# Sample attention by head in four column groups, and state-space outputs with channels on the rows

## The chip, the cores and the metric

One core of a Trainium2 chip runs the whole step. TensorE (PE in the profile, PEld its weight loads) multiplies; VectorE (DVE), ScalarE (ACT) and GpSimd (POOL) work elementwise; SyncE (SP) issues every DMA, in order. The metric is device microseconds of one execution. The kernel before was timed three times: 2014.14, 2015.0 and 2017.74 us, median 2015.0.

## The reference, cut to what matters

One layer of an encoder with four groups of heads that read one normalised input, for a prompt of 1024 rows and a sample of 32 rows (with a cache of 2048 past keys). Two groups matter here.

Group B is attention without softmax. Per head, with z = scale · q·k for every key before the query:

```
log_keep = where(mask, log_sigmoid(-z), 0)
suffix   = reverse_cumsum(log_keep) - log_keep
w        = where(mask, exp(log_sigmoid(z) + suffix), 0)
out      = w @ v          # 8 heads x 64
```

Group A is a state-space scan in chunks (8 heads of 64 channels in 2 groups of 4 heads, state of 128). Per chunk, with `acum` the running sum of dt·a, `decay` the causal exp(acum_t - acum_s), and h the state carried in:

```
y     = einsum('bthn,bshn,btsh,bshp->bthp', cc, bc, decay, xdt)
y    += einsum('bthn,bhpn,bth->bthp', cc, h, exp(acum))
h_new = exp(last) * h + einsum('bshn,bsh,bshp->bhpn', bc, w_s, xdt)
```

Afterwards y gets d_skip · x, is gated and normed, and the four groups go through one output projection and a layer norm.

## The kernel before, in words

The prompt is worked in two halves of 512 rows (`h` = 0, 1); the 32 sample rows go with the first. The input projection is 48 column tiles (`col_tile`, lines 351 to 353: three products of split operands per k), and these matmuls are the steady load of TensorE. `ORDER` and `weave` set what goes beside them: the second part of each unit (the attention blocks, the scan chunks and so on) is a generator, of which `weave` runs one step after every so many column tile steps. `follow` gives how many steps a generator has, so that they are spread evenly. After that the Tile scheduler orders the instructions of each engine, and each engine runs its own in that order.

`b_sample(gq)` (two calls, for heads 0 to 3 and 4 to 7; a pair of heads shares the 128 rows of a q, k or v tile) goes over the keys in five blocks, first the 32 new ones (`blk` 4), then four of 512. Its scores `zs` (line 917) hold four heads x 32 queries on 128 rows: the q tile `qb` of a pair is 128 x 128 with zeros outside its heads' places, and the two pairs add into one PSUM tile. `stick` makes weights `w` of it on ACT and DVE; `back` turns them (line 890) and multiplies (line 896) with v as the stationary operand, 128 x 128 for both heads of a pair, against 64 columns of weights, of which half of each product is not used.

`a_unit(h, g)` works a group of 4 heads in chunks of 128 rows (4 per half, and chunk 4 of 32 rows for the sample in the first half: 18 chunks in all for two groups and two halves). `weights` prepares a chunk: `bca` is the running sum copied to all rows by a DMA, three transposes `px` (lines 566 to 568), `xd` = x·dt (and a second version on POOL, line 572), `pg` = B·C (line 577), and `L`, the decay matrix of four heads: DVE, exp on ACT (line 584), product with `gt` on POOL (line 585). `outputs`, one step later, has the rows of the chunk on the partitions: four matmuls with `L` as the stationary operand against 64 columns (line 597), C against the state of 256 columns (line 600), two DVE operations that scale the second by exp(acum) and add (lines 605, 607), and the state update `pst` (line 609). `turn`, another step later, transposes y to channels on the rows (line 624) and adds d_skip · x (line 626). The loop has nch + 2 steps, 7 in the first half and 6 in the second. A group's second unit in a half is woven with the next half's first attention unit, and in the second half with the output projection (`prev`).

Of the kernel before, what the change touches and what calls it, by code (L numbers as in the profile page):

```python
# [6 lines left out]
F32 = mybir.dt.float32  # L7
F32R = mybir.dt.float32r
AF = mybir.ActivationFunctionType
ALU = mybir.AluOpType  # L10
# [52 lines left out]
def step_kernel(ctx, tc, xp, xs, cst, wmss, wmg, bgate, win, wsm, wout, lng, lnb, ck, cv,  # L63
# [320 lines left out]
    def narrow(h):  # L384
# [95 lines left out]
        for c in range(nch):  # L480
# [11 lines left out]
            A.activation(col[0:n, c, 24:32], col[0:n, c, 0:8], AF.Exp)  # L492
# [35 lines left out]
    def a_unit(h, g):  # L528
# [27 lines left out]
        def weights(c, n, cc):  # L556
# [30 lines left out]
            return L, xd, bt, el  # L587

        def outputs(c, n, cc, L, xd, bt, el):
            first = h == 0 and c == 0  # L590
            Hc = H
            if c == 4:
                Hc = sp.tile([P, 256], F32, tag="hs", name=nm("hs"), bufs=1)
                nc.sync.dma_start(Hc, ssmT[:, g * 256:(g + 1) * 256])
            py = ZT("py")
            for hh in range(4):
                T.matmul(py[0:n, hh * 64:(hh + 1) * 64], L[0:n, hh, 0:n], xd[0:n, 0, hh * 64:(hh + 1) * 64],  # L597
                         start=True, stop=True)
            if not first:
                T.matmul(py[0:n, 256:512], tiles["C"][:, cc], Hc, start=True, stop=True)  # L600
            y = WK("ya", [P, 2, 256])
            if first:
                V.tensor_copy(y[0:n, 0, :], py[0:n, 0:256])
            else:
                V.tensor_tensor(g4(y[0:n, 1, :], 4), g4(py[0:n, 256:512], 4),
                                col[0:n, c, 24 + 4 * g:28 + 4 * g].to_broadcast([n, 4, 64]), op=ALU.mult)
                V.tensor_tensor(y[0:n, 0, :], y[0:n, 1, :], py[0:n, 0:256], op=ALU.add)
# [11 lines left out]
            return y  # L619

        def turn(n, cc, y):
            pt = ST("pyt")
            for j in range(2):
                T.transpose(pt[:, j * P:j * P + n], y[0:n, 0, j * P:(j + 1) * P], ident[0:n, 0:n])
            for j in range(2):
                V.scalar_tensor_tensor(yg[j][:, cc], tiles[f"x{j}"][:, cc], C("dsk", 2 * g + j),
                                       pt[:, j * P:j * P + n], op0=ALU.mult, op1=ALU.add)

        todo1 = todo2 = None
        for c in range(nch + 2):  # L630
            done = todo2
            todo2 = None
            if todo1:
                todo2 = (*todo1[1:3], outputs(*todo1))
                todo1 = None
# [5 lines left out]
            if done:  # L641
                turn(*done)
# [920 lines left out]
```

## Time and profile before

| | before |
|---|---|
| median of three runs | 2015.0 us |
| profiled execution, its own time | 2011.09 us |
| its span from first to last instruction | 2009.2 us |
| TensorE busy | 1916.5 us (95%) |
| DVE, ACT, POOL busy | 1341.6, 767.0, 272.7 us |
| mean granted TensorE clock | 0.989 of full speed |

The span is the time from the first to the last instruction; the execution's own time has 1.9 us around it. Busy times of TensorE count modelled ends of matmuls that overlap, so what a matmul costs is read from the distance between starts, not from its own duration. A float32 matmul shows as two records, each with a weight load; the split operands of the projection are one record each, a transpose too.

### The profile page before, as it was taken

The page shows a single profiled execution, that of the slowest core. Times are in us where ns is not written, and L with a number is a line of the kernel's source. Part 1 is how long each engine was busy: PE and PEld are TensorE (multiplying, and loading weights), DVE is VectorE, ACT ScalarE, POOL GpSimd, SP SyncE. Part 2 cuts the span into 40 slices and gives each one's busy share as a digit, 9 for nine tenths or more (in the row PEclk, how much of TensorE's full clock was granted, in tenths as well). Part 3 has the DMA queues.
Part 4 walks back from the last instruction along what each step waited for, and adds up shares of the span by engine and source line. Part 5 has one row for each costly group of instructions (what it writes and reads, how often), then busy time and mean ns, then how long its engine had stood idle before and what let it go on. Part 6 is the DMA issues. An engine that isn't in the chain of part 4 may idle for free. (4 is left out here: it accounts for less than half of the span.)

```text
span 2009.2 us, 31503 instructions
## 1 busy us (share of the span) xinstructions
PE 1916.5 (95%) x11956; PEld 1599.0 (80%) x11956; DVE 1341.6 (67%) x2610; ACT 767.0 (38%) x1278; POOL 272.7 (14%) x481
## 2 busy tenths in 40 slices
PE   3999999999999999999999999999999999998998
PEld 1578999998889999977787886777878676676787
DVE  4325667877956857876678779876857664355765
ACT  5212533334464434435444444533334421133321
POOL 1000111202211202331101011121111210000000
PEclk9999999999999999999999999999999999999998
DMA  9786344333443343644232332433433635457733
GB/s 320 260 282 226 119 127 127 118 121 121 138 145 119 105 117 101 175 126 139 91 113 94 113 101 85 122 99 102 126 99 101 210 107 184 151 190 239 226 128 131
DMA packets 162031, 291.38 MB, mean 145 GB/s; under 512 B 23836, under 2 KB 66076, under 8 KB 161880
## 3 DMA queue, kind: packets, MB, share of 16 engines
q1 hardware_dynamic: 161880, 289.37, 45.3%
q8 instruction: 94, 1.54, 0.3%
q14 instruction: 57, 0.47, 0.1%
HBM read 253.49 MB, written 35.82 MB: 144 GB/s over the span
## 5 line engine op out<-in xcount | busy, mean ns | idle before, releaser
L351 PE MATMUL ip<-uh,wh 128*128 128x272 f32 (+4 forms) x2368 | 775.8, 328 | 0.4 <-POOL uh L277 0.4
L352 PE MATMUL ip<-ul,wh 128*128 128x272 f32 (+4 forms) x2368 | 765.6, 323 | 0.0
L353 PE MATMUL ip<-uh,wl 128*128 128x272 f32 (+4 forms) x2368 | 764.1, 323 | 0.0
L326 ACT CAST wh<-wr 128x1024 fp32r<-128x1024 f32 (+1 forms) x257 | 268.3, 1044 | 671.2 <-PE ip L352 404.8
L327 DVE TENSOR_TENSOR wl<-wr,wh 128x1024 fp32r<-128x1024 f32 (+1 forms) x257 | 314.6, 1225 | 253.8 <-ACT wh L326 239.4
L351 PEld LDWEIGHTS ip<-uh,wh 128*128 128x128 f32 x2368 | 449.5, 190 | 38.9 <-issue 7.7
L352 PEld LDWEIGHTS ip<-ul,wh 128*128 128x128 f32 x2368 | 449.4, 190 | 37.7 <-issue 7.0
L353 PEld LDWEIGHTS ip<-uh,wl 128*128 128x128 f32 x2368 | 449.3, 190 | 37.7 <-issue 7.3
L1241 PE MATMUL op<-wh,yh 128*128 128x512 f32 (+1 forms) x576 | 215.9, 375 | 7.6 <-DVE val L1252 7.6
L1243 PE MATMUL op<-wh,yl 128*128 128x512 f32 (+1 forms) x576 | 215.4, 375 | 0.0
L1242 PE MATMUL op<-wl,yh 128*128 128x512 f32 (+1 forms) x576 | 214.4, 372 | 0.0
L1103 DVE SCALAR_TENSOR_TENSOR cv<-cin,cs,cv 128x574 f32<-128x574 f32 (+1 forms) x240 | 187.4, 781 | 2.9
L1241 PEld LDWEIGHTS op<-wh,yh 128*128 128x128 f32 x576 | 109.0, 189 | 31.7 <-DVE val L1252 8.6
L1243 PEld LDWEIGHTS op<-wh,yl 128*128 128x128 f32 x576 | 109.0, 189 | 26.4 <-issue 7.3
L1242 PEld LDWEIGHTS op<-wl,yh 128*128 128x128 f32 x576 | 108.8, 189 | 22.3 <-issue 3.0
L1156 DVE SCALAR_TENSOR_TENSOR gacc<-wg,cs,gacc 128x512 f32<-128x512 f32 x120 | 89.1, 760 | 17.1 <-DMA wg<-in_wmg_dram 17.0
L804 POOL TENSOR_SCALAR_AFFINE_SELECT s<-s 128x128 f32<-128x128 f32 x64 | 35.4, 553 | 430.1 <-ACT s L702 429.8
L221 PE MATMUL mod<-wmr,cpad 128*32 128x512 f32 x256 | 38.2, 674 | 34.0 <-DMA wmr<-in_wmss_dram 34.0
L711 DVE TENSOR_TENSOR_SCAN pr<-kp 128x128 f32<-128x128 f32 (+4 forms) x66 | 54.0, 819 | 14.3 <-POOL kp L806 11.6
L702 ACT ACTIVATE s<-z 128x512 f32<-128x512 f32 (+3 forms) x96 | 47.7, 497 | 34.9 <-PE z L732 33.1
L715 DVE TENSOR_TENSOR s<-s,pr 128x512 f32<-128x512 f32 (+5 forms) x106 | 59.5, 564 | 2.0
L514 DVE SCALAR_TENSOR_TENSOR cv<-cin,cs,cv 128x547 f32<-128x547 f32 (+1 forms) x72 | 55.2, 767 | 0.3
(374 smaller groups left out, 2224.8 us busy)
## 6 DMA issues: line engine op xcount, KB each, us to landing
wr<-in_win_dram SPq DMA_DIRECT2D x192, 512.0 KB
wmr<-in_wmss_dram SPq DMA_DIRECT2D x128, 256.0 KB
wr<-in_wout_dram SPq DMA_DIRECT2D x63, 512.0 KB
wg<-in_wmg_dram SPq DMA_DIRECT2D x64, 256.0 KB
x<-in_xp_dram SPq DMA_DIRECT2D x32, 256.0 KB
out_dram<-val SPq DMA_DIRECT2D x32, 256.0 KB
xr<-in_xp_dram SPq DMA_DIRECT2D x28, 256.0 KB
yf<-ysc SPq DMA_DIRECT2D x16, 272.0 KB
```

What stands on the lines that cost most here:

```text
L326: A.copy(wh, wr)
L327: V.tensor_tensor(wl, wr, wh.bitcast(F32), op=ALU.subtract)
L351: T.matmul(pt[:, 0:n], wh[:, k % 8, :], uh[:, c0:c0 + n], start=(k == 0), stop=False)
L352: T.matmul(pt[:, 0:n], wh[:, k % 8, :], ul[:, c0:c0 + n], start=False, stop=False)
L353: T.matmul(pt[:, 0:n], wl[:, k % 8, :], uh[:, c0:c0 + n], start=False, stop=(k == KD - 1))
L514: V.scalar_tensor_tensor(acc[:, 0:n], t[:, i:i + n], C(wname, j * tap + i), acc[:, 0:n], op0=ALU.mult, op1=ALU.add)
L715: V.tensor_tensor(s[0:rows, 0:m], s[0:rows, 0:m], pr[0:rows, 1:m + 1], op=ALU.mult)
L1103: V.scalar_tensor_tensor(acc[:, 0:n], t[:, i:i + n], C("cdw", 31 * j + i), acc[:, 0:n], op0=ALU.mult, op1=ALU.add)
L1156: V.scalar_tensor_tensor(acc[j][:, 0:512], wr[:, 0:512], cT[:, k, j:j + 1], acc[j][:, 0:512], op0=ALU.mult, op1=ALU.add)
L1241: T.matmul(acc[t][:, 0:w], yh[:, c], wh, start=(first and i == 0), stop=False)
L1242: T.matmul(acc[t][:, 0:w], yh[:, c], wl, start=False, stop=False)
L1243: T.matmul(acc[t][:, 0:w], yl[:, c], wh, start=False, stop=(last and i == len(ws) - 1))
```

## The change

In `b_sample` the scores of each head become a matmul of their own: `qb` is 128 x 32, and head x uses its 64 rows of q and of k, and writes rows 32x to 32x + 31 of the same PSUM tile, so four matmuls of 64 rows x 32 columns stand in four column groups (order 2, 3, 0, 1). The values change sides: the turned weights (32 columns) are stationary, and v moves, 64 columns per head, in four column groups. The result has queries on the rows, so a copy, a transpose `yst`, a second copy and four small DMAs follow per call, where four copies and two DMAs stood.

In `a_unit` the outputs come with channels on the rows: `xd` (64 columns) is stationary and `L` moves; the state is stationary, and a new tile `ce` = C·exp(acum) moves (exp on ACT, product on POOL, in `weights`). Two heads stand in two column groups of 64. The two DVE operations, the two transposes, the tile `ya`, `turn` and one of the loop's steps go; d_skip · x is added from `py`. In a step `weights` of a chunk now stands before `outputs` of the chunk before it. `follow` and `prev` have one step less.

```diff
-            A.activation(col[0:n, c, 24:32], col[0:n, c, 0:8], AF.Exp)
...
-            return L, xd, bt, el
-
-        def outputs(c, n, cc, L, xd, bt, el):
+            if h == 0 and c == 0:
+                return L, xd, bt, el, None
+
+            ce = WK("ce", [P, 4, P])
+            A.activation(ce[:, :, 0:n], bca[:, :, 0:n], AF.Exp)
+            G.tensor_tensor(ce[:, :, 0:n], ce[:, :, 0:n], tiles["C"][:, None, cc].to_broadcast([P, 4, n]), op=ALU.mult)
+            return L, xd, bt, el, ce
+
+        def outputs(c, n, cc, L, xd, bt, el, ce):
...
             py = ZT("py")
-            for hh in range(4):
-                T.matmul(py[0:n, hh * 64:(hh + 1) * 64], L[0:n, hh, 0:n], xd[0:n, 0, hh * 64:(hh + 1) * 64],
-                         start=True, stop=True)
-            if not first:
-                T.matmul(py[0:n, 256:512], tiles["C"][:, cc], Hc, start=True, stop=True)
-            y = WK("ya", [P, 2, 256])
-            if first:
-                V.tensor_copy(y[0:n, 0, :], py[0:n, 0:256])
-            else:
-                V.tensor_tensor(g4(y[0:n, 1, :], 4), g4(py[0:n, 256:512], 4),
-                                col[0:n, c, 24 + 4 * g:28 + 4 * g].to_broadcast([n, 4, 64]), op=ALU.mult)
-                V.tensor_tensor(y[0:n, 0, :], y[0:n, 1, :], py[0:n, 0:256], op=ALU.add)
+            for j in range(2):
+                for st in range(1 if first else 2):
+                    for i in range(2):
+                        hh = 2 * j + i
+                        hc = slice(hh * 64, (hh + 1) * 64)
+                        if st == 0:
+                            x, m = xd[0:n, 0, hc], L[0:n, hh, 0:n]
+                        else:
+                            x, m = Hc[:, hc], ce[:, hh, 0:n]
+                        T.matmul(py[64 * i:64 * i + 64, j * P:j * P + n], x, m, start=st == 0, stop=first or st == 1,
+                                 skip_group_check=True)
+            for j in range(2):
+                V.scalar_tensor_tensor(yg[j][:, cc], tiles[f"x{j}"][:, cc], C("dsk", 2 * g + j),
+                                       py[:, j * P:j * P + n], op0=ALU.mult, op1=ALU.add)
...
-            return y
-
-        def turn(n, cc, y):
-            pt = ST("pyt")
-            for j in range(2):
-                T.transpose(pt[:, j * P:j * P + n], y[0:n, 0, j * P:(j + 1) * P], ident[0:n, 0:n])
...
-        for c in range(nch + 2):
...
+        for c in range(nch + 1):
+            done, todo = todo, None
...
-            qb = sp.tile([P, P], F32, tag="qb", name=nm("qb"), bufs=2)
-            G.memset(qb, 0.0)
-            o = (p % 2) * 64
-            G.tensor_copy(qb[0:64, o:o + 32], q[0:64, 512:544])
-            G.tensor_copy(qb[64:128, o + 32:o + 64], q[64:128, 512:544])
+            qb = sp.tile([P, SMP], F32, tag="qb", name=nm("qb"), bufs=2)
+            G.tensor_copy(qb, q[:, 512:544])
...
-                for j in range(2):
-                    lhs = prs[j][2] if blk == 4 else vc[j][:, b * P:(b + 1) * P]
-                    T.matmul(pa[:, 64 * j:64 * j + 64], lhs, wt[0:kn, b * P + 64 * j:b * P + 64 * j + 64],
-                             start=(blk == 4 and j == 0), stop=(blk == 0 and b == nb - 1), skip_group_check=True)
+                for x in range(4):
+                    v = prs[x // 2][2] if blk == 4 else vc[x // 2][:, b * P:(b + 1) * P]
+                    T.matmul(pa[32 * x:32 * x + 32, 0:64], wt[0:kn, b * P + 32 * x:b * P + 32 * x + 32],
+                             v[0:kn, 64 * (x % 2):64 * (x % 2) + 64], start=blk == 4, stop=blk == 0 and b == nb - 1,
+                             skip_group_check=True)
...
-            for j in range(2):
-                rhs = prs[j][1] if blk == 4 else kc[j][:, 0:512]
-                T.matmul(z[:, 0:n], prs[j][0], rhs, start=(j == 0), stop=(j == 1))
+            after = None
+            for x in (2, 3, 0, 1):
+                j, r = x // 2, slice(64 * (x % 2), 64 * (x % 2) + 64)
+                rhs = prs[j][1][r, :] if blk == 4 else kc[j][r, 0:512]
+                after = behind(T.matmul(z[32 * x:32 * x + 32, 0:n], prs[j][0][r, :], rhs,
+                                        start=True, stop=True, skip_group_check=True), after)
...
-        follow = {"A": (Au, 7 - h), "B": (B, 6 + 4 * h), "C": (Cu, 9 - 2 * h), "D": (Du, 11),
+        follow = {"A": (Au, 6 - h), "B": (B, 6 + 4 * h), "C": (Cu, 9 - 2 * h), "D": (Du, 11),
...
-        prev = [(chain(Au[1], a_finish(h)), 9 - h)]
+        prev = [(chain(Au[1], a_finish(h)), 8 - h)]
```

Three places in the order of instructions follow. A row has the line, the operation, output<-inputs and the output's size; numbers tell tiles of one name apart, and xN is N rows in a row that read the same.

TensorE, group 1's chunk 2 of the first half's scan, beside the first attention unit of the second half (`ip` is its column tile). Before:

```order
L609 MATMUL pst_10088<-xd_10033,bt_10036 128x256
L566 MATMUL px_10099<-ident,cv_9211 128x128
L567 MATMUL px_10099<-ident,cv_9478 128x128
L568 MATMUL px_10099<-ident,cv_8791 128x128
L351 MATMUL ip_10136<-uh_9866,wh_10126 128x512
L352 MATMUL ip_10136<-ul_9867,wh_10126 128x512
L353 MATMUL ip_10136<-uh_9866,wl_10127 128x512
L597 MATMUL py_10079<-xd_10033,L_10042 128x64 x4
L600 MATMUL py_10079<-hst_143,cv_9013 128x256
```

The same unit there after the change:

```order
L565 MATMUL px_10275<-ident,cv_9293 128x128
L566 MATMUL px_10275<-ident,cv_9515 128x128
L567 MATMUL px_10275<-ident,cv_8870 128x128
L576 MATMUL pg_10284<-cv_9095,cv_8870 128x128
L611 MATMUL py_10298<-L_10213,xd_10204 64x128 x2
L611 MATMUL py_10298<-ce_10220,hst_143 64x128 x2
L611 MATMUL py_10298<-L_10213,xd_10204 64x128 x2
L611 MATMUL py_10298<-ce_10220,hst_143 64x128 x2
L351 MATMUL ip_10325<-uh_9892,wh_10315 128x512
L617 MATMUL pst_10309<-xd_10204,bt_10207 128x256
```

The outputs of a chunk now stand right behind the transposes and `pg` of the next chunk, eight matmuls in one piece; from a chunk's `px` to its own `py` it is 40, 42, 37, 37 and 33 rows in the five chunks of this unit, where it was 32, 37, 36, 34 and 31, and to its `pst` 35 to 42 where it was 21 to 30. In the last unit of the kernel, beside the output projection, `px` to `py` is 48, 40, 38 and 33 rows where it was 51, 25, 26 and 31.

TensorE in the sample's attention, third block of the first call (`zs` scores, `wts` turned weights of the block before, `avs` values). Before:

```order
L917 MATMUL zs_5973<-kc_5965,qb_2156 128x512
L917 MATMUL zs_5973<-kc_5967,qb_3022 128x512
L890 MATMUL wts_5984<-ident,s_5774 128x128 x4
...
L896 MATMUL avs_5654<-wts_5989,vc_5767 128x64
L896 MATMUL avs_5654<-wts_5989,vc_5769 128x64
L896 MATMUL avs_5654<-wts_5989,vc_5767 128x64
L896 MATMUL avs_5654<-wts_5989,vc_5769 128x64
```

After:

```order
L913 MATMUL zs_5966<-kc_5960,qb_3015 32x512 x2
L913 MATMUL zs_5966<-kc_5958,qb_2151 32x512 x2
L881 MATMUL wts_5979<-ident,s_5765 128x128 x4
...
L888 MATMUL avs_5641<-vc_5756,wts_5984 32x64 x2
L888 MATMUL avs_5641<-vc_5758,wts_5984 32x64 x2
L888 MATMUL avs_5641<-vc_5756,wts_5984 32x64 x2
L888 MATMUL avs_5641<-vc_5758,wts_5984 32x64 x2
```

Two matmuls became four of 32 columns in the same place, for the scores and for each of the four 128-key pieces of the values; nothing stands between the four.

GpSimd, chunks 3 and 4 of the same scan unit as above. Before:

```order
L572 TENSOR_TENSOR xd_10185<-xd_10185,wss_10178 128x256
L585 TENSOR_TENSOR L_10194<-L_10194,gt_10192 128x512
L572 TENSOR_TENSOR xd_10260<-xd_10260,wss_10253 32x256
```

After:

```order
L571 TENSOR_TENSOR xd_10279<-xd_10279,wss_10272 128x256
L591 TENSOR_TENSOR ce_10295<-ce_10295,cv_9095 128x512
L584 TENSOR_TENSOR L_10288<-L_10288,gt_10286 128x512
L571 TENSOR_TENSOR xd_10361<-xd_10361,wss_10354 32x256
L591 TENSOR_TENSOR ce_10377<-ce_10377,cv_9095 128x4x32
```

The new product stands between a chunk's `xd` and its `L` in nine of the sixteen chunks that have it, as here; in four it is ahead of both, in three behind `L`.

## Rows read from the trace of the kernel before

**Rows 1.** The page: busy time of the engines, and the granted clock in 40 slices.

```profile
PE 1916.5 (95%) x11956; PEld 1599.0 (80%) x11956; DVE 1341.6 (67%) x2610; ACT 767.0 (38%) x1278; POOL 272.7 (14%) x481
...
PEclk9999999999999999999999999999999999999998
```

**Rows 2.** Waits of TensorE: us in total, times, longest us.

```profile
PE py L597 <- POOL L L585: 3.7, 6, 1.3
...
PE pst L609 <- POOL xd L572: 2.4, 3, 1.0
```

**Rows 3.** Windows: stretch, its us, engines' busy time; the sample's attention, the last scan.

```profile
500.00:650.00 150.00, 147.63 (x1071) 133.16 (x1069) 106.79 (x261) 77.58 (x132) 30.98 (x61) 1.00 0.44 135
...
1590.00:1625.00 35.00, 31.06 (x160) 23.55 (x159) 16.86 (x49) 9.22 (x21) 10.21 (x9) 0.95 0.25 75
```

**Rows 4.** Timeline of TensorE, sample attention: start, us from first start to last end, records.

```profile
522.74 1.89 PE L917 MATMUL zs<-kc,qb 128*128 128x512 f32 x4
524.47 0.60 PE L890 MATMUL wts<-ident,s 128*128 128x128 f32 x4
...
527.59 1.90 PE L896 MATMUL avs<-wts,vc 128*128 128x64 f32 x16
529.29 0.37 PE L351 MATMUL ip<-uh,wh 128*128 128x274 f32 x1
```

**Rows 5.** Timeline of TensorE, four column groups of 32 (conditioning, line 221).

```profile
113.23 0.29 PE L352 MATMUL ip<-ul,wh 128*128 128x272 f32 x1
113.36 0.29 PE L353 MATMUL ip<-uh,wl 128*128 128x272 f32 x1
113.58 1.06 PE L221 MATMUL mod<-wmr,cpad 128*32 128x512 f32 x8
114.57 0.39 PE L351 MATMUL ip<-uh,wh 128*128 128x272 f32 x1
```

**Rows 6.** Timeline of TensorE, two row halves: the prompt's scores, line 730.

```profile
955.57 0.39 PE L730 MATMUL z<-kh,qh 64*128 64x256 f32 x2
```

**Rows 7.** Timeline of TensorE, the scan's sample chunk.

```profile
828.67 0.63 PE L597 MATMUL py<-xd,L 32*32 32x64 f32 x8
829.23 0.62 PE L600 MATMUL py<-hs,cv 128*32 128x256 f32 x2
829.78 0.69 PE L609 MATMUL pst<-xd,bt 32*128 32x256 f32 x2
```

**Rows 8.** Timeline of TensorE, one chunk of 128 rows, and its transposes.

```profile
786.25 1.00 PE L597 MATMUL py<-xd,L 128*128 128x64 f32 x8
787.08 0.65 PE L600 MATMUL py<-hst,cv 128*128 128x256 f32 x2
787.57 0.59 PE L609 MATMUL pst<-xd,bt 128*128 128x256 f32 x2
...
795.12 0.44 PE L624 MATMUL pyt<-ident,ya 128*128 128x128 f32 x2
795.39 0.39 PE L1032 MATMUL pn<-v,W 128*128 128x129 f32 x2
```

**Rows 9.** Timeline of TensorE, two column groups of 64 (the prompt's values, line 843).

```profile
1102.39 0.28 PE L353 MATMUL ip<-uh,wl 128*128 128x258 f32 x1
1102.61 1.10 PE L843 MATMUL av<-wt,vt 128*64 128x128 f32 x16
1103.63 0.55 PE L828 MATMUL wt<-ident,s 128*128 128x128 f32 x3
```

**Rows 10.** Groups by line and shape: the scan's POOL product and ACT exp.

```profile
L585 POOL TENSOR_TENSOR L<-L,gt 128x512 f32<-128x512 f32 x16 | 20.7, 1296 | 18.6 <-ACT L L584 18.5
...
L584 ACT ACTIVATE L<-L 128x512 f32<-128x512 f32 x16 | 10.1, 631 | 11.3 <-DVE L L582 9.2 <-POOL xd L572 1.1 <-DVE dn L1046 0.9
```

**Rows 11.** Timeline of POOL, the scan unit beside the second half's first attention.

```profile
877.05 0.62 POOL L572 TENSOR_TENSOR xd<-xd,wss 128x256 f32<-128x256 f32 x1 [5.43 <-ACT wss L564]
879.01 1.27 POOL L585 TENSOR_TENSOR L<-L,gt 128x512 f32<-128x512 f32 x1 [1.34 <-ACT L L584]
```

More of the change, by code (lines that the diff above doesn't have):

```diff
@@ L618, in outputs @@
                 nc.sync.dma_start(o_ssmp[:, g * 256:(g + 1) * 256], Hc)
-            return y
-        def turn(n, cc, y):
-            pt = ST("pyt")
-            for j in range(2):
-                T.transpose(pt[:, j * P:j * P + n], y[0:n, 0, j * P:(j + 1) * P], ident[0:n, 0:n])
-            for j in range(2):
-                V.scalar_tensor_tensor(yg[j][:, cc], tiles[f"x{j}"][:, cc], C("dsk", 2 * g + j),
-                                       pt[:, j * P:j * P + n], op0=ALU.mult, op1=ALU.add)
-        todo1 = todo2 = None
-        for c in range(nch + 2):
[L631 to L635, printed above, removed]
+        todo = None
+        for c in range(nch + 1):
+            done, todo = todo, None
             if c < nch:
@@ L639, in a_unit @@
                 cc = slice(c0, c0 + n)
-                todo1 = (c, n, cc, *weights(c, n, cc))
+                todo = (c, n, cc, *weights(c, n, cc))
             if done:
-                turn(*done)
+                outputs(*done)
             yield 1
@@ L914, in b_sample @@
             z = ZT("zs")
-            for j in range(2):
-                rhs = prs[j][1] if blk == 4 else kc[j][:, 0:512]
-                T.matmul(z[:, 0:n], prs[j][0], rhs, start=(j == 0), stop=(j == 1))
+            after = None
[4 more added lines that the diff above has]
+                                        start=True, stop=True, skip_group_check=True), after)
             w, carry = stick(z[:, 0:n], P, n, diag if blk == 4 else None, carry)
@@ L923, in b_sample @@
         back(*todo)
-        for j in range(2):
-            ys = sp.tile([P, SMP], F32, tag="ysb", name=nm("ysb"))
-            for hh in range(2):
-                r = slice(64 * hh, 64 * hh + 64)
-                V.tensor_copy(ys[r], pa[r, 64 * j + 32 * hh:64 * j + 32 * hh + 32])
-            nc.sync.dma_start(ysc[0][4 + 2 * gq + j, :, 512:544], ys)
+        ys = sp.tile([P, 64], F32, tag="ysb", name=nm("ysb"), bufs=1)
+        V.tensor_copy(ys, pa[:, 0:64])
+        pt = ST("yst")
+        T.transpose(pt[0:64, 0:P], ys, ident)
+        yt = sp.tile([64, P], F32, tag="ysc", name=nm("ysc"), bufs=1)
+        V.tensor_copy(yt, pt[0:64, 0:P])
+        for x in range(4):
+            nc.sync.dma_start(ysc[0][4 + 2 * gq + x // 2, 64 * (x % 2):64 * (x % 2) + 64, 512:544],
+                              yt[:, 32 * x:32 * x + 32])
     def c_unit(h, hd):
```

## The prediction

> **What bounds the kernel now.** First the page: TensorE is busy 95% of the span, no other engine is above 67%, and the granted clock is full in nearly every slice [rows 1]. Then the windows. In the stretch that holds most of the sample's attention, TensorE works 147.6 of 150 us, so what is taken off its queue there shortens the run; in the last scan, beside the output projection, it works 31.1 of 35 us at 0.95 of the clock, so there it also waits [rows 3]. The waits say for what: `py` waits 3.7 us in six places for the POOL product that makes `L`, and `pst` 2.4 us in three for POOL's `xd` [rows 2]. With TensorE this full, a matmul costs the distance from its start to the next start, which the timeline of TensorE gives; its own duration overlaps its neighbours. So the sum is made of such distances, and of those waits.
>
> **Scores of the sample.** Per block of 512 keys there were two full matmuls, four records, 1.73 us from their start to the next one's [rows 4]. Now there are four of 64 rows x 32 columns. The nearest rows are the conditioning's: eight records of 512 columns in four column groups go from 113.58 to 114.57, that is 0.99 us, and they start 0.22 us after the projection's last record where 0.13 is usual [rows 5]. So entering and leaving that shape costs about 0.1 us each, and the four matmuls run at the same time: 1.08 us in all. That saves 0.65 us for each of 8 blocks (two calls of four), 5.2 us. What the rows don't show is two halves of rows that write one PSUM tile at the same time. Halves that write two tiles overlap: two records together take 0.39 us [rows 6], what one record alone has after such a change of shape [rows 5]. If they can't overlap in one tile, the four go in turn, because the written order alternates the halves: 4 x 0.865 (half of 1.73) + 0.2 = 3.66 us, a loss of 1.93 x 8 = 15.4 us. I take the 5.2, by the rows that are nearest in width and in rows, and keep both ends. The 32-key block of each call is short either way; I count nothing.
>
> The Trainium skill, TensorEngine Tiling (Array Packing), section Restrictions and Gotchas, says that different row tiles write different PSUM banks and cannot use the same one at a time. No run here shows that; by it the scores would lose the 15.4 us above.
>
> **Values of the sample.** Per block, 16 records (four pieces of 128 keys, two matmuls each) take 1.70 us [rows 4], 0.11 each: weights of 128 columns are loaded for a stream of only 64. Now it is 32 records, each with 32 columns of weights and 64 streamed columns. The trace has records of just that width in the scan's sample chunk, on one column group in turn: eight take 0.56 us, a change of shape included, 0.07 each [rows 7]. If four column groups overlap as they do at 512 columns [rows 5], a block is eight rounds of 0.07 plus 0.2, 0.76 us, and saves 0.94 x 8 = 7.5 us. If they don't, it is 32 x 0.07 + 0.2 = 2.44 us, a loss of 0.74 x 8 = 5.9 us. I take 7.5: in both shapes of column groups in the trace [rows 5, 9] the groups run together, and the loads of 32 columns go to different groups.
>
> The result needs a transpose per call now. With its change of shape I take 0.3 us, 0.6 in all (two plain ones take 0.27 [rows 8]). It waits for a copy on DVE, but eight projection records stand between, about 1 us, which covers a copy. The zero fills and copies that go from POOL, and the two more small DMAs per call on SyncE, are not on TensorE's path; the stores come some 1 us later, and the weight loads queued behind them run ahead of their use. I count nothing.
>
> **Scan outputs.** A chunk of 128 rows cost 0.83 us for the four `L` matmuls, 0.49 for the state's, and 0.27 for the transposes of y: 1.59 us [rows 8]. Now it is 16 records with 64 columns of weights and 128 streamed, in two column groups. That is the very shape of the prompt's values, of which the timeline has a piece of 16 records: from the record before, at 1102.39, to the record after, at 1103.63, 1.24 us, less 0.13 for the record before, 1.11 us with both changes of shape in it [rows 9]. So 0.48 us per chunk, and there are 14 of these (18 less two first and two sample chunks): 6.7 us. The two first chunks have no state part: 1.10 before, half of the 16 records and the same 0.2, about 0.66, now; 0.9 us. The sample chunk had 0.56 + 0.55 us [rows 7] and a short turn; its new form alternates 32 rows with 128, four pieces with a change of shape each, some 0.3 us apiece: nothing. Together 7.6 us, give or take 1.
>
> Off the path: DVE loses two operations per chunk, ACT gains an exp of `L`'s size, 0.63 us, and POOL a product of `L`'s size, 1.30 us [rows 10], for each of 16 chunks, some 10 and 20 us in engines that are busy 38% and 14% [rows 1].
>
> **The waits of the scan.** What they cost depends on whether `py` still comes after `L` and now `ce`. The order puts 33 to 48 TensorE rows between a chunk's `px` and its `py` in the two tight units, where it was 25 to 51, and 35 to 45 before `pst` where it was mostly 21 to 33: later than before in nearly every chunk. POOL's new product stands between `xd` and `L` in nine chunks. There POOL waited 1.34 us for the exp of `L` after `xd` [rows 11], so a product of 1.30 us just fits. Behind `py` and `pst` on TensorE stand the projection's matmuls, so a wait is paid in full; without that cover it is 1.3 x 9 = 11.7 us. I expect the room to win over the longer chain and take back half of the 6.1 us [rows 2], 3 us, between none and all; shorter waits also keep the clock up in the last scan, for which I add nothing.
>
> **The sum.** 5.2 + 7.5 - 0.6 + 7.6 + 3.0 = 22.7 us. The profiled execution took 2011.1 us of its own, 1.9 more than its span, so it would take 1988.4. The median of the runs is 3.9 us above it, so for the median 2015.0 - 22.7 = 1992.3 us. Some 0.2%, 4 us, is what a measurement of this kernel can tell from no change.
>
> **Rivals.**
> The values' groups don't gain at 64 columns, because loads and issue of 32 short records bind, not the array. For it: that width stands nowhere in four groups, and on one group 0.07 us is just what the record takes [rows 7]. Against it: the groups overlap elsewhere [rows 5, 9]. Gain nothing instead of 7.5: 1999.8 us; in turn: 2015.0 - (22.7 - 7.5 - 5.9) = 2005.7 us. Chance 0.15.
>
> The Trainium skill, TensorE: Matmul & The Clock Gate, section Back-to-back issue gap, gives about 62 ns per matmul when its instructions are decoded by microcode. By that a values block would be an estimated 32 x 0.062 + 0.2 = 2.18 us, a loss of 3.8 us in all; the rows fit it and do not show it.
>
> The scores' row halves go one after another in the shared PSUM tile: 22.7 - 5.2 - 15.4 = 2.1 us of gain, 2012.9 us. For it: the order alternates the halves, and no row shows them sharing a tile. Against it: they write different partitions, as the column groups do [rows 5], and halves overlap into two tiles [rows 6]. Chance 0.09; no change.
>
> Slower: POOL makes `py` late. `ce` on ACT and POOL, 0.63 + 1.30 us, stands ahead of `L`, and if none of it fits in idle time each of 16 chunks waits 1.93 us more: 30.9 us, and the 3 us are not given back, 2015.0 - 19.7 + 30.9 = 2026 us. It decides from (19.7 + 4) / 16 = 1.5 us per chunk. For it: `py` and `pst` already waited for POOL [rows 2]. Against it: POOL had idle time for it [rows 11], and the order gives more room. Chance 0.07.
>
> The rest, 0.05, is a matmul gain that another order of the neighbours (fetches, buffers) eats: 2011 to 2019 us.
>
> **How the numbers follow.** The likeliest, 0.64, is the sum: 1992, with its own range from 1984 (all waits gone, the values' rounds at 0.06) to 2000 (no wait given back, half of the values' gain). The range goes on to the case of the values in turn with a little less of the waits, 2008, and down to 1982: that leaves out the shared tile, POOL and the rest, about 0.2. Faster by over 0.2% is the likeliest, the values' case and a little of the rest: 0.81. Within 0.2%: the shared tile and part of the rest, 0.11. Slower: 0.08.
>
> **What would show it.** In the timeline after: the four score matmuls from start to next start near 1.1 us (1.7 or more if I am wrong, 3.6 for the shared tile); a values block near 0.8 us; a scan chunk's `py` in one piece of about 1.1 us, and no transposes of y. In the waits: `py` and `pst` for POOL at about 3 us in all, and nothing new of more than a few us; if POOL decides, `py` waiting for `L` or `ce` in most chunks, over 20 us. Wrong also if the tile `ce`, held for a step longer than the tile that it replaces, makes DMAs of `bca` wait for a buffer and with them the weights queued behind on SyncE: then the projection itself would wait for its weights, which it does nowhere now.

## The result and the profile after

| | before | after |
|---|---|---|
| median of four runs | 2014.9 us | 1995.5 us |
| lowest and highest run | 2014.1, 2017.7 us | 1990.7, 1996.0 us |
| profiled execution, its own time; span | 2011.09; 2009.2 us | 1990.74; 1989.0 us |

The ratio is 0.9896, 95% interval 0.9878 to 0.9914: 19.4 us of the median are gone (22.7 were forecast). The profiled execution of after was the shortest of its four, and lost 20.4 us against the profiled one of before.

The page of after, busy times, against [rows 1]: TensorE's busy time fell by 20.8 us, with more and shorter records; POOL gained 15 us, less than the 20 forecast. The 40 digits of the granted clock are the same as before.

```profile
PE 1895.7 (95%) x12194; PEld 1576.8 (79%) x12194; DVE 1340.7 (67%) x2572; ACT 774.1 (39%) x1287; POOL 287.6 (14%) x489
```

TensorE's timeline of after, the sample's attention, against [rows 4] (start, us from first start to last end, what, records):

```profile
528.10 0.29 PE L353 MATMUL ip<-uh,wl 128*128 128x274 f32 x1
528.32 0.65 PE L888 MATMUL avs<-vc,wts 128*32 128x64 f32 x32
528.90 0.40 PE L351 MATMUL ip<-uh,wh 128*128 128x274 f32 x1
...
533.16 0.30 PE L981 MATMUL ph<-ident,hn 128*128 128x128 f32 x1
533.39 1.06 PE L913 MATMUL zs<-kc,qb 64*32 64x512 f32 x8
534.39 0.66 PE L881 MATMUL wts<-ident,s 128*128 128x128 f32 x4
```

The scores go from 533.39 to 534.39, and start 0.23 us after `ph` where 0.11 is usual: about 1.1 us a block, as worked out. The values go from 528.10 to 528.90, less 0.13 for the record before: 0.67 us a block (1.70 before, 0.76 forecast). Within the block four records start some 7 ns apart, one in each column group, and the next four 56 ns after the first.

The same engine in a scan chunk of 128 rows, against [rows 8, 9]: from the projection's record at 1540.98 to `pst` at 1542.33 is 1.35 us, less 0.23 for that record: 1.12 us for outputs in one piece, 1.11 forecast. No transposes of y follow.

```profile
1540.98 0.40 PE L353 MATMUL ip<-uh,wl 128*128 128x512 f32 x1
1541.31 0.44 PE L611 MATMUL py<-L,xd 128*64 128x128 f32 x4
1541.57 0.39 PE L611 MATMUL py<-ce,hst 128*64 128x128 f32 x4
1541.79 0.39 PE L611 MATMUL py<-L,xd 128*64 128x128 f32 x4
1542.01 0.39 PE L611 MATMUL py<-ce,hst 128*64 128x128 f32 x4
1542.33 0.48 PE L617 MATMUL pst<-xd,bt 128*128 128x256 f32 x1
```

TensorE's waits in after, against [rows 2] (us in total, times, longest us):

```profile
PE ops L1233 <- DMA wr<-in_wout_dram: 7.5, 4, 2.6
...
PE py L611 <- POOL L L584: 2.3, 3, 1.2
...
PE pst L617 <- DVE gt L578: 1.4, 4, 0.5
...
PE pst L617 <- POOL xd L571: 1.3, 2, 1.0
...
PE zs L913 <- DMA kc<-in_ck_dram: 1.0, 1, 1.0
...
PE py L611 <- POOL ce L591: 0.4, 1, 0.4
```

Here the forecast fails. `py` and `pst` wait 5.4 us where it was 6.1. A row is new: `pst` waits for DVE's `gt`. It stands right behind `px` and `pg`, takes its tile from the same pool of two PSUM tiles, and that tile is free only when DVE has read `pg`. And `ops`, the sample's part of the output projection, waits 7.5 us for the weights w_out; before it was 4.7.

**Where the time went, by stage.** The first matmul of each group of three of the projection (line 351), and of the output projection behind it (line 1241), come in one order in all versions; the distance from the n-th to the m-th measures a stage. Each kernel was profiled twice (the second time as e10 and e11 below):

| stage, us | before | again | after | again |
|---|---|---|---|---|
| to the 769th such matmul | 450.3 | 450.0 | 451.1 | 450.7 |
| to the 1153rd: the sample's attention | 221.9 | 222.3 | 209.6 | 209.3 |
| to the 1345th | 81.8 | 81.8 | 81.8 | 81.8 |
| to the 1633rd: scan of the first half | 181.1 | 181.1 | 176.1 | 176.7 |
| to the 2209th | 503.8 | 503.2 | 503.4 | 502.4 |
| to the first `op`: first scan unit of the second half | 132.9 | 132.9 | 132.2 | 132.2 |
| to the end: output projection, beside the last scan | 437.3 | 444.7 | 434.8 | 444.5 |

(`op` is the output projection's matmul.) Up to the first `op` the change is worth 17.7 us (first pair) and 18.3 us (second pair). The last stage scatters by 7 to 10 us between executions of one kernel, and the pairs differ there by only 2.5 and 0.2 us. About half of that scatter is idle time of TensorE (3.8 us more in the second profile of before, 4.2 in that of after, of which `ops`'s wait for w_out is 2.0 and 1.7); the rest is the same number of matmuls with more busy time (3.6 and 5.5 us; the granted clock of the stage, the share of full speed that TensorE had, is 0.97 and 0.97 in before, 0.98 and 0.96 in after).

### The profile page after: what moved, and what is told of

The parts are those of the page before. It is cut to its first block, busy times and chain, and to the rows that moved or that the text cites. A ratio compares the mean times of both kernels' runs of the same rounds, so it can differ in the third digit from the quotient of the medians.

```text
span 1989.0 us, 31970 instructions
## 1 busy us (share of the span) xinstructions
PE 1895.7 (95%) x12194; PEld 1576.8 (79%) x12194; DVE 1340.7 (67%) x2572; ACT 774.1 (39%) x1287; POOL 287.6 (14%) x489
## 5 line engine op out<-in xcount | busy, mean ns | idle before, releaser
L706 DVE TENSOR_TENSOR_SCAN pr<-kp 128x128 f32<-128x128 f32 (+4 forms) x66 | 54.0, 818 | 14.8 <-POOL kp L797 12.1
L822 ACT COPY wt<-wt 128x512 f32<-128x512 f32 (+1 forms) x80 | 41.4, 563 | 38.5 <-PE wt L819 32.4
```

The lines of the kernel that those rows point to most:

```text
L706: V.tensor_tensor_scan(pr[0:rows, 0:nk][:, ::-1], kp[0:rows, 0:nk][:, ::-1], kp[0:rows, 0:nk][:, ::-1], initial=init, op0=ALU.mult, op1=AL ...
```

## The experiments

The theory after the result: the matmul terms are right and add up; the forecast's 3 us from waits don't come. Rivals: one of the terms is right by accident and another hides it; or the waits could have been given back but for one cause (the PSUM pool, the order in a step, POOL's new product, a queue, a buffer). Times of before beside them: median 2015.6 us for e1 to e4, 2015.8 for e5 to e8, 2017.5 for e9 to e11, 2018.6 for e12.

**e1, the sample's part alone; e2, the scan's part alone.** e1 has the new `b_sample` and the old `a_unit`, e2 the reverse.

```diff
# e1, taken back to before:
-            ce = WK("ce", [P, 4, P])
-                        T.matmul(py[64 * i:64 * i + 64, j * P:j * P + n], x, m, start=st == 0, stop=first or st == 1,
...
+                T.matmul(py[0:n, hh * 64:(hh + 1) * 64], L[0:n, hh, 0:n], xd[0:n, 0, hh * 64:(hh + 1) * 64],
# e2, taken back to before:
-            for x in (2, 3, 0, 1):
+                T.matmul(z[:, 0:n], prs[j][0], rhs, start=(j == 0), stop=(j == 1))
```

> The sample's attention is changed, the scan is as before. Theory (the gain is the distance between starts on TensorE): the stretch of the sample's attention gains what it gains in the whole change, 12.3 us between the last projection record before it and the first behind it, so 2014.9 - 12 = 2002.6 us, give or take 2. Rival (the order of the whole program made the gain, and the parts depend on each other): under 6 us or over 17 us, and the stretch of the sample's attention differs from that of the whole change.

> The scan is changed, the sample's attention is as before. Theory: the 8 us that the whole change gains behind the sample's attention, 2007 us, give or take 2; py pieces of 1.12 us, and pst waiting for DVE's gt in several places. Rival (parts depend on each other): under 4 or over 12 us.

Measured: e1 2006.3 us, ratio 0.9944 (0.9921 to 0.9966); its stage of the sample's attention takes 209.6 us, as in the whole change to a tenth. e2 2009.7 us, ratio 0.997 (0.9952 to 0.9989); its first-half scan stage takes 175.9 us, 5.2 less than before. So each stage's gain belongs to its own part: 0.56% and 0.30% make 0.86%, against 1.04% for both, within the intervals. Both runs gained less in all than their theories said (9.3 us for 12, 5.8 for 8), and more than their rivals allowed. e1 fell short of its expected time outside that stage (it reached the 769th matmul 4.0 us later than before, in a stage that the edit doesn't touch). Where e2 fell short isn't shown.

**e3, the scores alone; e4, the values' matmuls in turn.** e3 keeps the old values and the old scan. e4 is the changed kernel with the four pieces of 128 keys of one column group ahead of the next group's.

```diff
-            for b in range(nb):
-                for x in range(4):
+            for x in range(4):
+                for b in range(nb):
                     v = prs[x // 2][2] if blk == 4 else vc[x // 2][:, b * P:(b + 1) * P]
```

> Of the sample's attention the scores alone are changed; values and scan are as before. Theory: 1.09 us per block of scores against 1.73, so 5.1 us less, 2009.8 us. Rival (row halves that share a PSUM tile go in turn): 3.66 us per block, 15 us more, 2030 us. Second rival (the scores are cheaper, but the wait for their keys or weights takes it back): blocks of 1.1 us and a gain under 2 us.

> The changed kernel with the values' matmuls of a block in another order: all pieces of one head, then the next head, so that neighbours on the queue share a column group. Theory (what the values gain is the overlap of four column groups): 32 records in turn at about 0.056 us, some 2.0 us per block with the changes of shape instead of 0.67, 8 x 1.3 = 10.6 us more, 2006 us. Rival (the gain is from the shorter loads of 32 columns alone, or the queue finds the overlap whatever the order): blocks stay under 0.9 us and the time within 2 us of the changed kernel's 1995.5.

Measured: e4 2001.5 us, ratio 0.9933 (0.9907 to 0.9958). Its timeline:

```profile
529.50 0.29 PE L353 MATMUL ip<-uh,wl 128*128 128x274 f32 x1
529.71 1.40 PE L887 MATMUL avs<-vc,wts 128*32 128x64 f32 x32
531.04 0.39 PE L351 MATMUL ip<-uh,wh 128*128 128x274 f32 x1
```

A block takes 1.54 - 0.13 = 1.41 us, and the sample's stage 214.7 us, 5.2 more than in after. So of the values' 1.03 us per block, 0.29 stay when the groups come in turn, and 0.74 need the overlap of neighbours in different column groups. In turn it still beats the old form, which is where the rival of the forecast (2.44 us in turn) and e4's own theory (2.0 us) were wrong: records in turn follow each other in some 40 ns on average, not 70 or 56.

e3 took 2014.0 us, ratio 0.9992 (0.9972 to 1.0012): no gain that can be measured, the outcome of its second rival, though its scores blocks are as short as in after but for one. Its sample stage takes 219.9 us: 2.0 less than before, not 5.1. (In its profile the scan of the first half, which it leaves as it was, took 183.9 us, 2.8 more than before.) The waits and the windows of e3, and the window of before (us, busy time of PE, PEld, DVE, ACT, POOL, granted clock, DMA share, GB/s), show one place:

```profile
PE zs L916 <- DMA kc<-in_ck_dram: 1.7, 1, 1.7
```

```profile
553.30:558.00 4.70, 4.63 (x25) 3.27 (x26) 2.23 (x10) 3.02 (x7) 1.65 (x5) 0.64 0.24 60
```

```profile
553.30:558.00 4.70, 4.65 (x33) 4.12 (x34) 2.38 (x10) 2.99 (x6) 1.79 (x8) 1.00 0.32 91
```

TensorE waits 1.7 us for the keys (0.7 before), and behind that wait the granted clock is 0.64 of full speed on average, part of the stretch at 1.2 GHz instead of 2.4: 0.36 of 4.7 us, 1.7 us, are lost to it. In after the wait is 1.0 us and the clock behind it stays full. The wait alone doesn't explain the loss: it is 1.3 us in the second profile of before, and 1.8 us in e6 below, whose sample stage takes 210.0 us all the same. What only e3 has here is the lower clock, and that is one profile.

**e12, the old scores in the changed kernel**, asks the same from the other side.

```diff
-            qb = sp.tile([P, SMP], F32, tag="qb", name=nm("qb"), bufs=2)
-            G.tensor_copy(qb, q[:, 512:544])
+            qb = sp.tile([P, P], F32, tag="qb", name=nm("qb"), bufs=2)
+            G.memset(qb, 0.0)
...
-            for x in (2, 3, 0, 1):
+                T.matmul(z[:, 0:n], prs[j][0], rhs, start=(j == 0), stop=(j == 1))
...
-        ys = sp.tile([P, 64], F32, tag="ysb", name=nm("ysb"), bufs=1)
+        ys = WK("ysb")[:, 0:64]
```

> The changed kernel with the scores of before (two full matmuls per block, q tiles with zeros); the values in four column groups and the scan's new outputs stay (for room, two small tiles of the result stand in the pool wk). Theory (the values' gain is the distance from start to start, 8 blocks x 1.03 us, less the transposes, and the scores' 5 us come on top only together with it, because in the scores-only run a wait for the keys of 1.7 us and a clock of 0.64 behind it took 3 us back): the sample's attention gains 7 to 8.5 us against before, the wait for the keys is 0.7 to 1.3 us, and the run is 4 to 5 us longer than the changed kernel: 2000. Rival (the two gains do not add: the scores bring 2 us there whatever the values do, since what TensorE saves at the scores it waits for later): the sample's attention gains 10 us or more, and the run is 2 us longer than the changed kernel or less: 1997.5.

Measured: 2008.6 us, ratio 0.9944 (0.9923 to 0.9965), and 220.4 us for the sample's stage: a gain of 1.5 us, below what either theory gave. The values' own distances are those of after. Waits stand in the stage that after does not have, in e12's list for 455 to 675 us:

```profile
PE zs L913 <- DMA kc<-in_ck_dram: 2.1, 1, 2.1
...
PE pq L952 <- DMA wq<-in_wqkv_dram: 0.9, 2, 0.5
PE wts L884 <- DVE s L710: 0.8, 1, 0.8
PE yst L923 <- DVE ysb L921: 0.8, 1, 0.8
PE zs L913 <- PE ip L351: 0.7, 1, 0.7
```

The windows of this stage tell work from waiting. They are those of before again, after, e3 and e12, in this order, with the columns as above:

```profile
450.00:672.30 222.30, 216.52 (x1604) 198.20 (x1603) 161.74 (x362) 109.32 (x185) 46.35 (x81) 0.99 0.40 124
451.10:660.70 209.60, 202.91 (x1783) 183.00 (x1781) 159.15 (x357) 109.27 (x185) 44.86 (x77) 0.99 0.42 132
451.00:670.90 219.90, 213.08 (x1645) 194.51 (x1644) 160.86 (x362) 109.40 (x185) 44.44 (x77) 0.98 0.40 126
454.60:675.00 220.40, 209.41 (x1743) 188.01 (x1741) 161.20 (x357) 110.71 (x186) 44.66 (x81) 0.99 0.40 125
```

Against before again, TensorE's busy time falls by 13.6 us in after, by 7.1 in e12 (the values alone; 8.2 less two transposes were due) and by 3.4 in e3 (the scores alone), or 5.1 with the 1.7 us that the lower clock cost there. So the work nearly adds up, 12.2 of 13.6 us. What doesn't add up is the idle time: TensorE is idle 5.8 us in before again, 6.7 in after and 6.8 in e3, but 11.0 in e12, which takes 5.2 of its 7.1 us back. The 4.3 us that it has more than after are the rows above: 1.1 us more for the keys, and 3.2 us of waits that after does not have. The two tiles in the other pool also moved the projection's and the linear attention's matmuls around the blocks, so this run doesn't show whether the old scores or those tiles made these waits.

**e5 to e7, what `py` and `pst` wait for.** e5 puts `pst` into the free half of `py`'s PSUM tile; e6 puts `outputs` ahead of `weights` in a step, as before; e7 makes `ce` on DVE.

```diff
# e5
-            pst = ST("pst")
-            T.matmul(pst[:, 0:256], bt[0:n], xd[0:n, 1, :], start=True, stop=True)
+            pst = py[:, 256:512]
+            T.matmul(pst, bt[0:n], xd[0:n, 1, :], start=True, stop=True, skip_group_check=True)
# e6
             done, todo = todo, None
+            if done:
+                outputs(*done)
             if c < nch:
# e7
-            G.tensor_tensor(ce[:, :, 0:n], ce[:, :, 0:n], tiles["C"][:, None, cc].to_broadcast([P, 4, n]), op=ALU.mult)
+            V.tensor_tensor(ce[:, :, 0:n], ce[:, :, 0:n], tiles["C"][:, None, cc].to_broadcast([P, 4, n]), op=ALU.mult)
```

> The changed kernel, but the state update pst is written into the free half of py's own PSUM tile (256 columns right behind py's pieces), so it takes no buffer of the two-buffer pool that px and pg use. Theory (pst waits for that pool: its buffer is free only when DVE's gt has read pg): the rows 'pst <- DVE gt' (1.4 us, 4 times in the changed kernel) vanish, py and pst waits together go from 5.4 to 4 us or less, the scan unit beside the second half's first attention gains some 1.9 us against before where the whole change gains 0.64 there, and the run is 1 to 2 us shorter than the changed kernel, about 1994 as a median, too little for the times to tell. Rival 1 (the wait only changes its name: what holds pst back is the late chunk as a whole, bt or xd): pst waits for ACT's or POOL's operation instead, the unit gains 0.6 as before. Rival 2 (py's tile is now read later, so the next py or score waits for it): waits of 1 us or more for the two-buffer pool of py, no gain or a loss of 1 to 3 us.

> The changed kernel, but in a step of the scan the outputs of the chunk before stand ahead of the preparation of this one, as in the kernel before. So the distance on TensorE from px to the same chunk's py is shorter and pst no longer stands right behind px and pg. Theory (of the two orders, the new one gives the long chain of POOL its time, and only pst pays for it): the waits of py for POOL grow from 2.7 us in the changed kernel to 4 to 8, those of pst for DVE's gt (1.4 us) vanish, and the run is 1 to 5 us longer, median 1996 to 2001. Rival (the order does not matter for POOL, only for pst): py's waits stay within 1 us of 2.7, pst's 1.4 vanish, and the run is 1 to 2 us shorter.

> The changed kernel, but the product C times exp(acum), ce, is made by DVE instead of POOL, 16 products. Theory (POOL's new product holds up L, and with it py, in those chunks where it stands between xd and L): the waits of py and pst for POOL, 2.3, 0.4 and 1.0 us, fall by half or more, and the run is 1 to 2 us shorter unless DVE, 67% busy, gives it back. Rival (POOL waits for the exp anyway, so its product costs nothing, and py's waits are for a chain that begins at DVE and ACT): the waits for POOL stay at 3 to 4.5 us or turn into waits of about the same size for DVE, and the run is within 2 us of the changed kernel; if DVE's 16 x about 0.6 us delays the stick-breaking or the weight splits, 1 to 5 us longer.

Measured: e5 1999.1 us, ratio 0.9915 (0.9885 to 0.9945); e6 1995.1, 0.9893 (0.9874 to 0.9912); e7 1998.5, 0.9911 (0.9892 to 0.9929). None differs from the change itself by more than the intervals. The waits of e5, e6 and e7, in this order:

```profile
PE py L611 <- POOL L L584: 5.9, 4, 2.0
...
PE py L611 <- POOL ce L591: 0.7, 2, 0.4
```

```profile
PE py L611 <- POOL L L584: 4.4, 6, 1.1
...
PE pst L617 <- POOL xd L571: 1.2, 2, 0.8
```

```profile
PE py L611 <- POOL L L584: 2.1, 4, 0.6
...
PE pst L617 <- DVE gt L578: 1.3, 2, 0.8
...
PE pst L617 <- POOL xd L571: 0.9, 2, 0.5
```

In e5 the wait of `pst` for `gt` is gone, as the theory said, and `py` waits 6.6 us where it was 2.7: more in all, not less. It also costs more than the wait: the stage of the first half's scan takes 179.7 us in e5, 3.6 more than in after, and holds two waits of `py` for `L`, 2.0 us at 848 us and 1.7 at 858, each with a lower granted clock behind it. These are e5's windows there; in after the clock is full in the whole stage:

```profile
850.00:855.00 5.00, 5.00 (x21) 3.91 (x19) 3.18 (x11) 0.47 (x2) 0.00 (x0) 0.66 0.63 194
860.00:865.00 5.00, 4.59 (x23) 3.40 (x24) 1.41 (x7) 0.20 (x1) 2.70 (x3) 0.66 0.50 160
```

In e6 the wait for `gt` is gone too, and `py` waits 1.7 more; 5.6 in all. In e7 POOL is relieved of 16 products, and 4.3 us stay, 3.0 of them for POOL. So the wait for `gt` is shown to come from the place of `pst` and from its pool. The sums show less, because they scatter: profiles with the new scan as it is have 5.4 us (after), 6.9 (e11), 7.0 (e2), 4.9 (e4), 3.5 (e8), 3.9 (e9) and 6.2 (e12), and 6.6, 5.6 and 4.3 lie among them. That the chain from `px` over DVE, ACT and POOL to `L` is about as long as the matmuls that TensorE has for that time, so that the order decides who waits at its end, fits these runs and is not shown by them.

**e8 and e9, the wait for w_out.** e8 takes eight of the sixteen loads `yf`, which stand between the weights' loads on SyncE's queue, to POOL's queue. e9 gives the raw weights three buffers, and the io tiles 18 for 20.

```diff
# e8
-        nc.sync.dma_start(yf[:, 0:n], ysc[h][k, :, 0:n])
+        (nc.gpsimd if h == 0 and k > 7 else nc.sync).dma_start(yf[:, 0:n], ysc[h][k, :, 0:n])
# e9
-        wr = wp.tile(shape, F32, tag="wr", name=nm("wr"), bufs=2)
+        wr = wp.tile(shape, F32, tag="wr", name=nm("wr"), bufs=3)
```

> The changed kernel, but the second eight of the sixteen loads yf, which bring the mixers' outputs back ahead of the output projection, are issued by POOL's queue instead of SyncE's, so that the loads of w_out are not queued behind one that waits for a buffer. Theory (the longer wait of the output projection's ops for its weights, 7.5 us where it was 4.7, comes from this queue: a pair of yf issues stood 3.8 us ahead of the second block's load): the first wait of ops, 2.6 us, falls below 1.5, the sum to 5.5 or less, the stretch from the last scan's begin gains the 4 us that op lost, partly (1 to 3 us), and the run is 1 to 3 us shorter. Rival (the weights wait for their own two buffers, which ops' matmuls free, and for bandwidth: the DMA engines are 83 to 94% busy there): the wait stays at 6 to 8 us and the run is within 2 us of the changed kernel.

> The changed kernel with three buffers instead of two for the raw weights wr, and 18 instead of 20 for the io tiles to make room. Theory (ops waits for w_out because ops itself reads the raw block, so that both buffers are still held when the next block should be fetched; moving the loads to another queue therefore did not help): the wait of ops for wr goes from 7.5 us (12.1 with the loads moved) to 3 or less, the time is 2 to 5 us shorter than the changed kernel's, 1991 to 1994. Rival 1 (bandwidth: the DMA engines are 83 to 94% busy where the output projection begins, with mixers' outputs as well as weights): the wait stays at 5 us or more and the time within 2 us of 1995.5. Rival 2 (two tiles fewer in io hold up the loads of keys and values or the inputs of the mixers): the wait for the keys, 1.0 us, grows by 1 us or more, or new waits for DMA of more than 2 us appear; 2 to 10 us longer.

Measured: e8 2001.2 us, ratio 0.9927 (0.9909 to 0.9945); e9 1997.7, 0.9902 (0.987 to 0.9933). Both theories fell. The waits of e8, then of e9:

```profile
PE ops L1233 <- DMA wr<-in_wout_dram: 12.1, 5, 6.9
```

```profile
PE ops L1233 <- DMA wr<-in_wout_dram: 10.9, 7, 5.0
```

Moving half of `yf` off the queue does not shorten the wait for the weights, and neither does a third buffer. In e9 the first three blocks' `ops` go through in one piece, and the fourth then waits 5.0 us. One suspect is the transfers themselves: in after, from 1557 to 1572 us, the DMA engines are busy 83% of the time, and TensorE 11.3 of 15 us. But before has an even higher share in the same place, 0.90, with TensorE busy 14.5 of 15 us (after, then before):

```profile
1557.00:1572.00 15.00, 11.29 (x66) 7.49 (x65) 9.55 (x14) 7.36 (x12) 4.06 (x10) 1.00 0.83 279
```

```profile
1575.00:1590.00 15.00, 14.45 (x85) 9.45 (x84) 9.86 (x14) 8.52 (x13) 4.94 (x9) 1.00 0.90 266
```

So a busy share of the DMA engines alone doesn't make the wait, and no run here took those transfers away: why `ops` waits longer stays open.

**e10 and e11, both kernels unchanged, a second time.**

> The kernel before, unchanged, profiled a second time. Theory (the 4.7 us that the output projection's ops waited for w_out in its first profile are what this kernel waits): 4 to 5.5 us again, and the stretch from the last scan to the end within 1 us of the first profile. Rival (this wait scatters from execution to execution, and the first profile of before had a small one): 6 us or more, or a stretch that differs by 2 us or more; then the 4 us that op lost in the changed kernel's last scan are no effect of the change.

> The changed kernel, unchanged, profiled a second time; the first profile was the shortest of its four runs (1990.7 us, the median 1995.5). Theory (the matmul work and the scan's waits repeat, DMA waits scatter): the sample's attention gains 12.3 us against before within 0.2, py and pst wait 5 to 6 us in all for POOL and DVE, and what is longer by some 3 to 5 us stands in the waits for DMA, at the start or in the output projection. Rival (the waits of the scan scatter too): py and pst wait below 4 or above 7 us.

Measured: 2017.84 and 1999.21 us. The stages are in the table above. The waits of before again, then of after again:

```profile
PE ops L1233 <- DMA wr<-in_wout_dram: 6.7, 7, 2.4
...
PE py L597 <- POOL L L585: 3.7, 6, 1.3
...
PE pst L609 <- POOL xd L572: 2.5, 3, 1.0
```

```profile
PE ops L1233 <- DMA wr<-in_wout_dram: 9.2, 6, 3.9
...
PE pst L617 <- DVE gt L578: 2.7, 5, 0.9
PE py L611 <- POOL L L584: 2.7, 4, 1.1
PE pst L617 <- POOL xd L571: 1.1, 1, 1.1
...
PE py L611 <- POOL ce L591: 0.4, 1, 0.4
```

`py` and `pst` waited 6.1 and 6.2 us in the two profiles of before and 5.4 and 6.9 in those of after. With the runs above, the four profiles with the old scan (e1 and e3 have 6.2 and 6.4) have a mean of 6.2 us, and the seven with the new scan as it is 5.4, from 3.5 to 7.0: some 0.8 us were given back, a quarter of the forecast. The wait for w_out scatters by 2 us, as e10's rival said, and yet there is a shift: the four profiles with the old scan have 4.7, 6.7, 5.0 (e1) and 5.2 (e3), the eight with the new scan and untouched loads (after, e11, e2, e4 to e7, e12) 7.1 to 9.2. The means are 5.4 and 8.0.

## Why the prediction was right, and where it was off

The time, 1995.5 us, lies in the range and 3.2 us above the forecast of 1992.3.

- **Scores**, 5.2 us: 0.64 us for each of 8 blocks, 5.1, by the timeline. The row halves that write different partitions of one PSUM tile run together, which no row had shown; the rival of the shared tile is out. The Trainium skill, TensorEngine Tiling (Array Packing), section Restrictions and Gotchas, has it that row tiles can't use one PSUM bank at the same time; the trace disagrees, eight records of both row halves into different partitions of one tile take 1.0 us.
- **Values**, 7.5 us: 1.03 us a block, 8.2. The forecast took 0.07 us for a round of four, and it is 0.056. e4 shows that the overlap of the groups gives 5.9 of it, so the rival that 32 short records bind is out. The Trainium skill, TensorE: Matmul & The Clock Gate, section Back-to-back issue gap, gives 62 ns per matmul when microcode decodes it; here a record comes every 0.67 / 32 = 21 ns, and a matmul of two records every 42, so that does not bind this block.
- Scores, values and transposes together: 12.1 forecast, 12.3 and 13.1 in the table's pairs. By e3 and e12 the work of the two parts nearly adds up; alone, each lost most of its gain, in e3's profile partly to a lower clock and in e12's to waits, and the forecast had no term for either.
- **Scan outputs**, 7.6 us: the piece of 1.11 us measured 1.12. Of the term, 0.9 + 6 x 0.48 + 4 x 0.48 = 5.7 us lie ahead of the first `op`, and the stages there (first-half scan and first unit of the second half) gained 5.7 and 5.1, though the waits of `py` and `pst` in them grew (2.2 us before, both times; 3.4 and 3.9 after). The agreement is partly luck: 3.8 us were due in the first half's scan, which gained 5.0 and 4.4, and 1.9 in the second half's unit, which gained 0.7 both times with only 0.2 us of such waits in it. Which cost the forecast missed there isn't shown. The last 1.9 us lie beside the output projection.
- **The waits of the scan** are the step that failed: "I expect the room to win over the longer chain and take back half of the 6.1 us, 3 us". It measured 0.7 less in one pair and 0.7 more in the other, and 0.8 less on average over all profiles: too large by some 2.2 us. Beside the output projection these waits did fall, from 3.9 and 4.0 us to 2.0 and 3.0; ahead of it they grew by 1.2 and 1.7. The room was there, more rows between `px` and `py`, but the new place put `pst` right behind `px` and `pg`, where it needs a PSUM tile that DVE still reads, a wait that I did not look for (1.4 and 2.7 us). e5 and e6 show that this wait goes with its cause, and that the sum doesn't fall with it: 6.6 and 5.6 us stay.
- **The last scan** then gave little: the last stage gained 2.5 and 0.2 us, with 1.9 of matmuls and half of the waits forecast for it. `ops` waits some 2.6 us more for w_out where the scan beside it is the new, shorter one. Why isn't shown: e8 and e9 didn't shorten it, and the DMA share doesn't set it apart from before.
- The rival of a slower run (POOL makes `py` late, over 20 us of waits) did not come: 2.7 us stand at `py`. Nor did DMAs of `bca` delay the projection's weights.

So of the 3.2 us between forecast and median some 2.2 are the waits' term, which was too large. The rest can't be placed: the last stage alone scatters by more. The matmul terms were right to about 1 us as sums; by stage the scan's are off by up to 1.2 both ways.

## What to carry to other kernels

Cost a matmul that fills only part of the array by the distance from start to start of the nearest shape in the trace, with one change of shape in and one out; that gave each piece here (a block of scores or values, a chunk's outputs) to a tenth of a microsecond. What a stage gains can still differ by a microsecond or so. Don't count a wait as given back because there is more room ahead of it: ask which buffer, from which pool, the waiting instruction needs, and who reads it last. And where a saving stands ahead of a wait (the keys in e3, w_out in the last scan), the wait and a lower clock behind it can take part of it back; split a stage into busy time, idle time and granted clock before saying that two gains don't add up. Profile one kernel several times before reading a difference of a few us: here the waits of `py` and `pst` alone went from 3.5 to 7.0 us with the same scan.

## What the hardware did that I had not expected

The same wait had different prices. `av`, the prompt's values, waits 2.7 to 2.8 us for ACT's turned weights `wt` near 476 us in all versions; in the profile of before the clock stayed full behind it, in that of after it fell to 0.51 for the next 3 us, nearly all of it at 1.2 GHz (before, then after; columns as above):

```profile
479.00:482.00 3.00, 3.00 (x26) 3.00 (x25) 0.59 (x2) 1.29 (x2) 0.00 (x0) 1.00 0.34 92
```

```profile
479.00:482.00 3.00, 3.00 (x15) 3.00 (x15) 1.28 (x3) 1.06 (x2) 0.00 (x0) 0.51 0.13 33
```

It is not the change: before again has 0.73 in the same stretch. Some 1.6 us are lost at that place: the projection's records come that much later in before again than in before, and within 20 us both are level again; in between before has 1.1 us of waits (`pq` and `pk`, two small projections) that the other doesn't have. In e3 and e5 the time lost behind a wait did not come back within the stage. The other surprise is the rate of small matmuls: four column groups of 32 take a new record every 21 ns on average, entry and exit included, and in turn, one group after the other, every 40 ns or so.
